# Last two of sixteen experts: rows of the sums fetched ahead, adds on VectorE, and the last expert in two groups of columns

## The chip, the cores and the metric

The kernel runs on one core of a Trainium2 chip. Time is device time in microseconds for one launch. TensorE (PE) does matrix products, VectorE (DVE) and ScalarE (ACT) work on elements, GpSimd (POOL) here mostly issues indirect DMAs, and SyncE (SP) issues loads. Each engine runs its instructions in the order in which the program lists them, and waits at one whose inputs aren't ready.

## The reference

One decoder layer on 2048 tokens of width 1024: a mixer (pooling and gated linear attention), then a mixture of 16 small experts. The change touches only the second half:

```python
def hier_moe(x, w_rg, b_rg, w_re, b_re, w_gate, w_up, w_down):
    ...   # each token: one group of 4 experts, two experts of that group, two weights
    for e in range(N_EXPERTS):
        h = jax.nn.silu(xt @ w_gate[e]) * (xt @ w_up[e])
        y = y + combine[:, e:e + 1] * (h @ w_down[e]).astype(f32)
    return y
# then, after h = h + hier_moe(rmsnorm(h)):
    return rmsnorm(h, final_norm_w)[:, N_META:]
```

Each expert has 256 hidden values. Both experts of a token are in the same group of four, so its row is complete after the later one of the two; then comes the final norm (a sum of squares over the row, a reciprocal root, a scaling) and the store.

## The kernel before, in words

Experts run one after the other, `e` from 0 to 15. Each takes up to 320 tokens (`CAP`), in three blocks of rows: `j` = 0 and 1 of 128 tokens, `j` = 2 of 64. As columns of the transposed tokens they stand in the order 2, 0, 1: columns 0 to 64, 64 to 192, 192 to 320 (`cols`). All values are split in a high and a low part, so that each product is three matmuls.

An expert has these steps. `gate_up`: for each half `f` of the hidden values, 8 blocks of 3 matmuls for the gate and 8 for the up matrix, 128 hidden values by 320 tokens each. The four sums go to PSUM banks: gate of `f` 0, up of `f` 0 and gate of `f` 1 to the tag `mm`, which has two banks taken in turn, up of `f` 1 to the tag `m2`, which has one. Then ScalarE does Silu into the one tile `h`, VectorE multiplies by the up sum, and `split_hidden` makes the high part (ScalarE) and the low part (VectorE) in `HB`. `down`: six units, one for each block `j` and half `a` of the 1024 outputs, each three matmuls of 512 columns for each `f` (two for `j` = 2 before the last expert, which packs its parts); first all units for `f` 0, then all for `f` 1. `evac` brings each unit into the row tile `xr`.

The running sums of the tokens lie in a DRAM array, `oe`. Before the change experts 0 to 14 do it thus: ScalarE copies the unit with the token's weight; an indirect DMA adds the rows of those tokens for which this expert is the first to `oe`; another adds the rows of `oe` to the tile, for those for which it is the second. `square` (ScalarE) sums the squares, `finish` takes the reciprocal root by a seed and three Newton steps on VectorE (`seed_rstd`, L51 to L67) and scales the row (L997), and `store` writes it to the output. Expert 15 is second for all its tokens: its three row tiles are fetched from `oe` while its gate products run (`between`, i = 1), and `evac` (L969) multiplies and adds on VectorE. Expert 14 is finished row block by row block (`finish_row`) from `between` of expert 15 (i = 4). For blocks 0 and 1 of expert 15, GpSimd multiplies by the final norm's weight (L1018) and ScalarE by the reciprocal root (L1023); block 2 goes through VectorE (L997).

There are six row tiles `xr` (`RB`), three for an expert, so that expert 15 takes those of expert 13 once these are stored. The order on each engine is made by a scheduler when the program is built, from dependences and priorities. The parts in `tc.high_priority()` are to be placed early; where they stand in the end only the list of the engine's instructions tells.

Of the kernel before, what the change touches and what calls it, by code (L numbers as in the profile page):

```python
# [7 lines left out]
F32 = mybir.dt.float32  # L8
F32R = mybir.dt.float32r
BF = mybir.dt.bfloat16  # L10
I32 = mybir.dt.int32
AF = mybir.ActivationFunctionType
# [57 lines left out]
def body(ctx, tc, I, O):  # L70
# [760 lines left out]
    with ExitStack() as c2:  # L831
# [54 lines left out]

        def gate_up(e, between):
            for f in range(2):
                ps = []
                for b in range(2):  # L890
                    p = bank(("mm", "m2")[f * b])
                    c = slice(b * 256 + f * 128, b * 256 + f * 128 + 128)
                    for k in range(KB):
                        if k % 4 == 0:
                            between(f * 4 + b * 2 + k // 4)
                        wh, wl = gate_slot(e, k)[0][:, c], gate_slot(e, k)[1][:, c]
                        xh, xl = XE[e % 2][k]
                        nc.tensor.matmul(p[:, :CAP], wh, xh, start=(k == 0), stop=False)  # L898
                        nc.tensor.matmul(p[:, :CAP], wh, xl, start=False, stop=False)  # L899
                        nc.tensor.matmul(p[:, :CAP], wl, xh, start=False, stop=(k == KB - 1))  # L900
                    ps.append(p)
                with tc.high_priority():
                    h = me.tile([128, CAP], F32, name="h")
                    nc.scalar.activation(h, ps[0][:, :CAP], AF.Silu)
                    V.tensor_tensor(h, ps[1][:, :CAP], h, op=OP.mult)
                    split_hidden(HB[:, f], h, 0, CAP)

# [34 lines left out]
        def down(e, js=(0, 1, 2)):  # L942
            le = e % 4
            if e < NE - 1 and e not in RT:
                RT[e] = [row_tile(True) for j in range(3)]
            tags = ("sp", "o", "ds", "tp", "zg", "m2") if e else ("mm", "mm", "ds", "m2", "ds", "m2")
            units = [(j, a, bank(tags[2 * j + a])) for j in js for a in range(2)]

# [15 lines left out]
            def evac(u):  # L964
                j, a, p = u
                n, c = rows[j], slice(a * 512, a * 512 + 512)
                x, w = RT[e][j][:n, c], col(e, j, 3, True)
                if e == NE - 1:
                    V.scalar_tensor_tensor(x, p[:n], w, x, op0=OP.mult, op1=OP.add)  # L969
                else:  # L970
                    nc.scalar.activation(x, p[:n], AF.Copy, scale=w)  # L971
                if j == 2 and e < NE - 1:
                    V.scalar_tensor_tensor(x, p[64:128], w, x, op0=OP.mult, op1=OP.add)
                x = RT[e][j]
                if a and le < 3:
                    add_oe(e, ind(oe, x[:n], col(e, j, 1), True, add=True), False)
                if a and le and e < NE - 1:
                    add_oe(e, ind(x[:n], oe, col(e, j, 2), False, add=True), True)
                if a and e == NE - 1:
                    finish_row(e, j)  # L980
# [32 lines left out]
        def finish_row(e, j):  # L1013
            n, x = rows[j], RT[e][j]
            square(e, j)
            if e == NE - 1 and j < 2:
                z = row_tile()
                nc.gpsimd.tensor_tensor(z[:n], x[:n], fw[:n], op=OP.mult)  # L1018
            ms = mk.tile([128, 1], F32, name="msl", bufs=3)
            V.scalar_tensor_tensor(ms[:n], SS[e % 2][:n, part[j]:part[j] + 1], SCALE / D, col(e, j, 4, True), op0=OP.mult, op1=OP.add)  # L1020
            r = seed_rstd(nc, mk, ms[:n], 1, n)
            if e == NE - 1 and j < 2:
                nc.scalar.activation(z[:n], z[:n], AF.Copy, scale=r)  # L1023
                store(e, j, z)
            else:
                scale_out(e, j, r)

# [24 lines left out]
        fw = mk.tile([128, D], F32, name="fw")  # L1052
        must_follow(nc.sync.dma_start(fw, I["fnw"].partition_broadcast(128)), first_rows)
        SS = [mk.tile([128, 3], F32, name=f"SS{i}") for i in range(2)]
        for i in range(2):
# [15 lines left out]
        for e in range(NE):  # L1071
            def between(i):
# [7 lines left out]
                else:  # L1080
                    for _ in range((e + 1 < NE) + (i < 4)):
                        gate = stream[done[0]][0] == "g"
                        for op in split_chunk():
                            if gate:
                                must_follow(op, hidden_done)
                        load_chunks(done[0] + WRB, mk)
                if e == NE - 1 and i == 1:
                    RT[e] = [row_tile(True) for j in range(3)]
                    for j, n in enumerate(rows):
                        add_oe(e, ind(RT[e][j][:n], oe, col(e, j, 0), False), True)  # L1090
                if i == 4 and e == NE - 1:
                    for j in range(3):
                        finish_row(e - 1, j)
            if e > 1:
# [147 lines left out]
```

## Time and profile before

| | us |
|---|---|
| median of 3 runs (1138.27 to 1140.39) | 1139.0 |
| the profiled execution | 1135.03 |
| its span, from the first to the last instruction | 1133.3 |
| TensorE busy, whole span | 1084.9 |
| VectorE busy, whole span | 790.1 |
| ScalarE busy, whole span | 583.3 |
| GpSimd busy, whole span | 290.8 |

The span is made of very different stages, so the busy times of the whole say little on its end. The profile's timeline gives each instruction's start, its duration, its line and tiles, and in brackets how long the engine stood idle ahead of it and what ended that. TensorE's matmuls overlap, so that the step from one start to the next is what one costs, not its duration. The granted clock of TensorE (PEclk) is 1.00 at 2.4 GHz and 0.50 at 1.2 GHz.

### The profile page before, as it was taken

To read this page: it belongs to the slowest core of one execution; us is meant where nothing else is said; L and a number is where in the kernel's file an instruction comes from. 1 tells how busy PE (TensorE), PEld (TensorE's weight loads), DVE (VectorE), ACT (ScalarE), POOL (GpSimd) and SP (SyncE) were. 2 spreads that over 40 slices of the span, in tenths; PEclk is the share of its full clock that TensorE was granted. 3 is DMA by queue.
4 is the path that set the end of the run, shared out by engine and by line. 5 is a ranking of instruction groups with operands and counts; after the bars stand their busy time and mean duration, and the time that the engine had idled before them with its cause. 6 is when DMAs were issued, how large, how long until landed. Compare 5 with 4: busy or idle time off the path is not lost. (4 is left out here: it accounts for less than half of the span.)

```text
span 1133.3 us, 19603 instructions
## 1 busy us (share of the span) xinstructions
PE 1084.9 (96%) x6748; PEld 974.0 (86%) x6748; DVE 790.1 (70%) x2706; ACT 583.3 (51%) x1286; POOL 290.8 (26%) x261
## 2 busy tenths in 40 slices
PE   6999999999999999999999997999999999999991
PEld 4888888888888889999999996679999889999980
DVE  6476666545554876777887887567886778688664
ACT  7545444344434733333333434477775777677541
POOL 2000000000000000111111126336645645564363
PEclk9999999999999999999999999999999999999996
DMA  7412323111211542343343535598999899799532
GB/s 267 172 66 75 117 89 102 48 56 62 69 66 57 177 158 99 127 150 141 112 150 103 178 134 175 166 307 209 245 270 258 215 275 288 181 254 275 155 72 75
DMA packets 75576, 175.41 MB, mean 155 GB/s; under 512 B 15283, under 2 KB 15716, under 8 KB 75472
## 3 DMA queue, kind: packets, MB, share of 16 engines
q1 hardware_dynamic: 48848, 105.73, 29.2%
q0 software_dynamic: 24032, 59.83, 20.1%
q10 hardware_dynamic: 2592, 8.55, 1.9%
q8 instruction: 55, 0.90, 0.3%
q14 instruction: 49, 0.40, 0.1%
HBM read 142.96 MB, written 52.76 MB: 173 GB/s over the span
## 5 line engine op out<-in xcount | busy, mean ns | idle before, releaser
L420 POOL DMA_DIRECT2D y_dram<-y x16 | 8.6, 540 | 392.7 <-DVE y L418 392.7
L849 POOL DMA_INDIRECT oe<-xr,tab x36 | 59.2, 1643 | 97.9 <-ACT xr L971 91.0
L300 PE MATMUL mm<-wb,XL 128*128 128x512 f32 (+1 forms) x240 | 83.6, 348 | 0.0
L301 PE MATMUL mm<-wb,XH 128*128 128x512 f32 (+1 forms) x240 | 83.1, 346 | 0.0
L299 PE MATMUL mm<-wb,XH 128*128 128x512 f32 (+1 forms) x240 | 82.3, 343 | 0.0
L653 POOL DMA_INDIRECT table<-rec,ix x32 | 33.5, 1045 | 179.6 <-DVE sv_all L669 142.8
L499 PE MATMUL mm<-XH,ws 128*128 128x256 f32 (+1 forms) x256 | 73.3, 287 | 0.1
L500 PE MATMUL mm<-XL,ws 128*128 128x256 f32 (+1 forms) x256 | 72.9, 285 | 0.0
L501 PE MATMUL mm<-XH,ws 128*128 128x256 f32 (+1 forms) x256 | 72.4, 283 | 0.0
L849 POOL DMA_INDIRECT xr<-oe,tab x36 | 57.6, 1599 | 22.9 <-ACT xr L971 12.8
L110 DVE TENSOR_TENSOR wb<-raw,wb 128x512 fp32r<-128x512 f32 x83 | 55.4, 686 | 9.4 <-ACT wb L109 8.5
L109 ACT ACTIVATE XH<-xt 128x1024 fp32r<-128x1024 f32 x32 | 33.9, 1058 | 49.4 <-PE mm L501 26.4
L109 ACT ACTIVATE wb<-raw 128x512 fp32r<-128x512 f32 x91 | 55.1, 624 | 4.4 <-DVE ix L636 1.8
L898 PE MATMUL mm<-xh,ws 128*128 128x320 f32 x168 | 53.4, 318 | 0.0
L900 PE MATMUL mm<-xh,ws 128*128 128x320 f32 x168 | 53.0, 316 | 0.0
L899 PE MATMUL mm<-xl,ws 128*128 128x320 f32 x168 | 52.6, 313 | 0.0
L991 ACT ACTIVATE sq<-xr 128x1024 bf16<-128x1024 f32 (+1 forms) x36 | 37.8, 1049 | 22.5 <-DMA xr<-oe,tab 8.1
L299 PE MATMUL mm<-ws,XH 128*128 128x512 f32 x112 | 47.4, 423 | 2.0 <-ACT XH L109 2.0
L299 PEld LDWEIGHTS mm<-wb,XH 128*128 128x128 f32 x240 | 45.3, 189 | 4.4
L301 PEld LDWEIGHTS mm<-wb,XH 128*128 128x128 f32 x240 | 45.2, 188 | 4.5
L300 PEld LDWEIGHTS mm<-wb,XL 128*128 128x128 f32 x240 | 45.2, 189 | 4.3
L499 PEld LDWEIGHTS mm<-XH,ws 128*128 128x128 f32 x256 | 47.9, 188 | 0.9 <-ACT XH L109 0.6
(615 smaller groups left out, 3946.6 us busy)
## 6 DMA issues: line engine op xcount, KB each, us to landing
raw<-in_wgu_e_dram SPq DMA_DIRECT2D x86, 256.0 KB
xt<-in_xT_dram SPq DMA_DIRECT2D x32, 512.0 KB
xn<-in_xn_dram SPq DMA_DIRECT2D x32, 512.0 KB
raw<-in_wd_e_dram SPq DMA_DIRECT2D x48, 256.0 KB
wr<-in_wgu_e_dram SPq DMA_DIRECT2D x42, 256.0 KB
hn_dram<-xn ACTq DMA_DIRECT2D x16, 512.0 KB
oe<-xn POOLq DMA_DIRECT2D x16, 512.0 KB
raw<-in_wrest_dram SPq DMA_DIRECT2D x16, 256.0 KB
```

Source lines behind the costliest of these rows:

```text
L109: return (nc.scalar.activation(hi, src, AF.Copy), (eng or V).tensor_tensor(lo, src, hi.bitcast(F32), op=OP.subtract))
L110: (eng or V).tensor_tensor(lo, src, hi.bitcast(F32), op=OP.subtract))
L299: nc.tensor.matmul(q, xh[:, k, :], wh[:, c0:c1_], start=(k == 0), stop=False)
L300: nc.tensor.matmul(q, xl[:, k, :], wh[:, c0:c1_], start=False, stop=False)
L301: nc.tensor.matmul(q, xh[:, k, :], wl[:, c0:c1_], start=False, stop=(k == KB - 1))
L499: nc.tensor.matmul(ps[:, b], WS[k][0][:, c], XH[:, k, o:], start=(k == 0), stop=False)
L500: nc.tensor.matmul(ps[:, b], WS[k][0][:, c], XL[:, k, o:], start=False, stop=False)
L501: nc.tensor.matmul(ps[:, b], WS[k][1][:, c], XH[:, k, o:], start=False, stop=(k == KB - 1))
L849: return nc.gpsimd.indirect_dma_start(out=out_, out_offset=off if scatter else None, in_=in_, in_offset=None if scatter else off, bounds_c ...
L898: nc.tensor.matmul(p[:, :CAP], wh, xh, start=(k == 0), stop=False)
L899: nc.tensor.matmul(p[:, :CAP], wh, xl, start=False, stop=False)
L900: nc.tensor.matmul(p[:, :CAP], wl, xh, start=False, stop=(k == KB - 1))
```

## The change

Experts 14 and 15 (`ahead`) now both fetch their rows of `oe` into the row tiles ahead of their `down`, and `evac` multiplies and adds on VectorE (L971 of the changed kernel). Expert 14 then writes the rows for which it is the first to `oe` as they are, without adding, and no longer reads `oe` back. The squares of both are taken by half rows in `evac` (L984), into `SL`. `finish_row` adds the halves and scales on VectorE for all blocks; the multiplication on GpSimd is gone. Expert 15 goes through `gate_up` by columns: first 0 to 192 (blocks 2 and 0) for both `f`, then 192 to 320 (block 1) for `f` 0, then `down` of blocks 0 and 2, then columns 192 to 320 for `f` 1, and `down` of block 1.

```diff
-        def gate_up(e, between):
-            for f in range(2):
+        def gate_up(e, between, fs=(0, 1), c0=0, c1_=CAP):
+            for f in fs:
...
-                        xh, xl = XE[e % 2][k]
-                        nc.tensor.matmul(p[:, :CAP], wh, xh, start=(k == 0), stop=False)
+                        xh, xl = (x[:, c0:c1_] for x in XE[e % 2][k])
+                        nc.tensor.matmul(p[:, c0:c1_], wh, xh, start=(k == 0), stop=False)
...
                 with tc.high_priority():
                     h = me.tile([128, CAP], F32, name="h")
-                    nc.scalar.activation(h, ps[0][:, :CAP], AF.Silu)
-                    V.tensor_tensor(h, ps[1][:, :CAP], h, op=OP.mult)
-                    split_hidden(HB[:, f], h, 0, CAP)
+                    nc.scalar.activation(h[:, c0:c1_], ps[0][:, c0:c1_], AF.Silu)
+                    V.tensor_tensor(h[:, c0:c1_], ps[1][:, c0:c1_], h[:, c0:c1_], op=OP.mult)
+                    split_hidden(HB[:, f], h, c0, c1_)
...
             tags = ("sp", "o", "ds", "tp", "zg", "m2") if e else ("mm", "mm", "ds", "m2", "ds", "m2")
+            tags = ("sp", "o", "ds", "sp", "zg", "tp") if e == NE - 1 else tags
+            ahead = e >= NE - 2
...
-                if e == NE - 1:
+                if ahead:
                     V.scalar_tensor_tensor(x, p[:n], w, x, op0=OP.mult, op1=OP.add)
                 else:
                     nc.scalar.activation(x, p[:n], AF.Copy, scale=w)
...
                 if a and le < 3:
-                    add_oe(e, ind(oe, x[:n], col(e, j, 1), True, add=True), False)
-                if a and le and e < NE - 1:
+                    add_oe(e, ind(oe, x[:n], col(e, j, 1), True, add=not ahead), False)
+                if a and le and not ahead:
                     add_oe(e, ind(x[:n], oe, col(e, j, 2), False, add=True), True)
+                if ahead:
+                    h = slice(a * 512, a * 512 + 512)
+                    sq = mk.tile([128, D], BF, name="sq")
+                    nc.scalar.activation(sq[:n, h], RT[e][j][:n, h], AF.Square, accum_out=SL[e % 2][:n, j, a:a + 1])
...
         def finish_row(e, j):
-            n, x = rows[j], RT[e][j]
-            square(e, j)
-            if e == NE - 1 and j < 2:
-                z = row_tile()
-                nc.gpsimd.tensor_tensor(z[:n], x[:n], fw[:n], op=OP.mult)
-            ms = mk.tile([128, 1], F32, name="msl", bufs=3)
-            V.scalar_tensor_tensor(ms[:n], SS[e % 2][:n, part[j]:part[j] + 1], SCALE / D, col(e, j, 4, True), op0=OP.mult, op1=OP.add)
-            r = seed_rstd(nc, mk, ms[:n], 1, n)
-            if e == NE - 1 and j < 2:
-                nc.scalar.activation(z[:n], z[:n], AF.Copy, scale=r)
-                store(e, j, z)
-            else:
-                scale_out(e, j, r)
+            n, q = rows[j], SL[e % 2][:rows[j], j]
+            ms = mk.tile([128, 1], F32, name="msl", bufs=3)[:n]
+            V.tensor_scalar(ms, q[:, 0:1], q[:, 1:2], SCALE / D, op0=OP.add, op1=OP.mult)
+            V.tensor_tensor(ms, ms, col(e, j, 4, True), op=OP.add)
+            scale_out(e, j, seed_rstd(nc, mk, ms, 1, n))
...
-                if e == NE - 1 and i == 1:
+                if e >= NE - 2 and i == 1 and e not in RT:
                     RT[e] = [row_tile(True) for j in range(3)]
                     for j, n in enumerate(rows):
                         add_oe(e, ind(RT[e][j][:n], oe, col(e, j, 0), False), True)
-                if i == 4 and e == NE - 1:
-                    for j in range(3):
-                        finish_row(e - 1, j)
+                if i == 4 and e == NE - 1 and e - 1 not in OUT:
+                    OUT[e - 1] = [finish_row(e - 1, j) for j in range(3)]
+            if e == NE - 1:
+                gate_up(e, between, (0, 1), 0, 192)
+                gate_up(e, between, (0,), 192, CAP)
+                down(e, (0, 2))
+                gate_up(e, between, (1,), 192, CAP)
+                down(e, (1,))
+                break
```

How the built order moves is seen in the lists of instructions. In them `h` is the tile of hidden values, `HB` its split, `msl` and `sr_y` belong to the reciprocal roots, `mm` and `m_...` are the banks of gate and up, `sp`, `o`, `ds` are banks of `down`; the numbers behind a name tell buffers apart.

VectorE, the first hidden values of expert 15, before: they stand behind the conversion of the last down weights and the first step of one reciprocal root.

```order
L110 TENSOR_TENSOR wb_105<-wr,wb_104 128x512
L1020 SCALAR_TENSOR_TENSOR msl<-SS_8915,tab 128x1
L905 TENSOR_TENSOR h<-mm,h 128x320
L58 TENSOR_SCALAR sr_y<-msl 128x1
L59 TENSOR_SCALAR sr_y<-sr_y 128x1
```

The same place after the change:

```order
L66 SCALAR_TENSOR_TENSOR sr_y<-sr_t,sr_y 64x1
L1003 SCALAR_TENSOR_TENSOR xr<-xr,sr_y,fw 64x1024
L905 TENSOR_TENSOR h<-mm,h 128x192
L883 TENSOR_TENSOR HB<-h,HB 128x128
L885 TENSOR_TENSOR HB<-h,HB 128x64
L905 TENSOR_TENSOR h<-m_13546,h 128x192
```

The first multiplication now stands behind the whole end of expert 14: the row that scales its last block (64x1024) is the one ahead of it. Between the last split of expert 14's hidden values and this multiplication stand 60 instructions: 8 adds, 4 conversions, 6 scalings and 42 small ones.

TensorE, the end of expert 15's gate and up products, before: `down` follows at once.

```order
L898 MATMUL m_13535<-xh_8712,wb_100 128x320
L899 MATMUL m_13535<-xl_8713,wb_100 128x320
L900 MATMUL m_13535<-xh_8712,wb_101 128x320
L957 MATMUL sp<-wb_102,HB 128x512
L958 MATMUL sp<-wb_102,HB 128x512
```

After, at the end of the first group of columns:

```order
L898 MATMUL m_13546<-xh_8712,wb_100 128x192
L899 MATMUL m_13546<-xl_8713,wb_100 128x192
L900 MATMUL m_13546<-xh_8712,wb_101 128x192
L898 MATMUL mm<-wb_106,wb_94 128x128
L899 MATMUL mm<-wb_107,wb_94 128x128
```

Two sums of 128 columns, 48 matmuls, now stand between the first group's hidden values and `down`, and the first of them takes the `mm` bank that the first up sum of the group was in.

VectorE near the end, before: the six units of `down` come one after the other, with the roots among them.

```order
L969 SCALAR_TENSOR_TENSOR xr<-ds,tab,xr 128x512
L969 SCALAR_TENSOR_TENSOR xr<-tp,tab,xr 128x512
L1020 SCALAR_TENSOR_TENSOR msl<-SS_8916,tab 128x1
L969 SCALAR_TENSOR_TENSOR xr<-zg,tab,xr 64x512
L58 TENSOR_SCALAR sr_y<-msl 128x1
```

After, the last hidden values and the last two units:

```order
L1003 SCALAR_TENSOR_TENSOR xr<-xr,sr_y,fw 64x1024
L905 TENSOR_TENSOR h<-m_13731,h 128x128
L883 TENSOR_TENSOR HB<-h,HB 128x128
L971 SCALAR_TENSOR_TENSOR xr<-ds,tab,xr 128x512
L971 SCALAR_TENSOR_TENSOR xr<-sp,tab,xr 128x512
L1022 TENSOR_SCALAR msl<-SL_8916 128x1
```

The last hidden multiplication stands behind the scaling of blocks 0 and 2, and only block 1 is left behind it.

## Rows read from the trace of the kernel before

**Rows 1.** Windows, whole core: from:to, length; busy us (count) by engine; clock, DMA
```profile
1082.43:1096.70 14.27, 14.21 (x97) 13.94 (x95) 9.34 (x21) 5.77 (x11) 12.13 (x8) 1.00 0.48 65
1096.70:1108.90 12.20, 10.44 (x36) 7.16 (x36) 10.95 (x32) 3.76 (x10) 10.06 (x9) 0.86 0.60 177
1099.70:1102.90 3.20, 3.20 (x9) 2.51 (x9) 2.92 (x11) 0.92 (x2) 2.69 (x2) 0.51 0.51 140
1108.90:1120.45 11.55, 0.00 (x0) 0.00 (x0) 9.26 (x30) 4.44 (x6) 6.60 (x5) 0.69 0.18 66
```
**Rows 2.** Timeline of TensorE, experts 14 and 15: start, duration, instruction [idle before]
```profile
1079.19 0.40 PE L959 MATMUL sp<-wb,HB 128*128 128x512 f32 x1
...
1082.43 0.31 PE L898 MATMUL mm<-wb,wb 128*128 128x320 f32 x1
...
1096.33 0.31 PE L900 MATMUL m<-xh,wb 128*128 128x320 f32 x1
...
1098.96 0.50 PE L958 MATMUL sp<-wb,HB 128*128 128x512 f32 x1 [1.08 <-DVE HB L883]
...
1104.56 0.39 PE L957 MATMUL sp<-wb,HB 128*128 128x512 f32 x1
...
1108.49 0.40 PE L959 MATMUL m<-wb,HB 128*64 128x512 f32 x1
```
**Rows 3.** Timeline of ScalarE: squares of expert 14 and expert 15
```profile
1090.76 1.06 ACT L991 ACTIVATE sq<-xr 128x1024 bf16<-128x1024 f32 x1 [4.18 <-DMA xr<-oe,tab]
...
1106.98 1.06 ACT L991 ACTIVATE sq<-xr 128x1024 bf16<-128x1024 f32 x1 [3.41 <-DVE xr L969]
```
**Rows 4.** Timeline of VectorE from 1080 us on
```profile
1080.76 0.17 DVE L1008 SCALAR_TENSOR_TENSOR ms<-SS,tab 128x3 f32<-128x3 f32 x1 [0.35 <-ACT sq L991]
...
1083.16 1.29 DVE L997 SCALAR_TENSOR_TENSOR xr<-xr,sr_y,fw 128x1024 f32<-128x1024 f32 x1
...
1085.82 2.47 DVE L997 SCALAR_TENSOR_TENSOR xr<-xr,sr_y,fw 128x1024 f32<-128x1024 f32 x2
1088.20 1.29 DVE L110 TENSOR_TENSOR wb<-raw,wb 128x512 fp32r<-128x512 f32 x2
...
1092.13 0.49 DVE L905 TENSOR_TENSOR h<-mm,h 128x320 f32<-128x320 f32 x1
...
1105.47 0.73 DVE L969 SCALAR_TENSOR_TENSOR xr<-sp,tab,xr 128x512 f32<-128x512 f32 x1
1106.14 0.75 DVE L969 SCALAR_TENSOR_TENSOR xr<-o,tab,xr 128x512 f32<-128x512 f32 x1
...
1108.69 3.81 DVE L1020 SCALAR_TENSOR_TENSOR msl<-SS,tab 128x1 f32<-128x1 f32 x1
...
1113.81 0.13 DVE L59 TENSOR_SCALAR sr_y<-sr_y 128x1 int32<-128x1 int32 x1
...
1117.09 1.28 DVE L997 SCALAR_TENSOR_TENSOR xr<-xr,sr_y,fw 64x1024 f32<-64x1024 f32 x1
```
**Rows 5.** Timeline of GpSimd: a gather with addition, the multiplications, the last store
```profile
1084.03 1.85 POOL L849 DMA_INDIRECT xr<-oe,tab  x1 [0.30 <-issue]
...
1107.78 4.70 POOL L1018 TENSOR_TENSOR xg<-xr,fw 128x1024 f32<-128x1024 f32 x2
...
1119.53 0.92 POOL L849 DMA_INDIRECT out_dram<-xr,tab  x1 [0.30 <-issue]
```
**Rows 6.** DMA, 1055 to 1080 us: busy tenths in 40 slices of 0.625 us
```profile
DMA  7998668996799897559775410000000000000000
```
**Rows 7.** Timeline of TensorE earlier: 128 columns at full clock, 256 at half
```profile
199.73 0.39 PE L389 MATMUL o<-v,sc 128*128 128x128 f32 x2
...
200.18 0.39 PE L389 MATMUL o<-v,sc 128*128 128x128 f32 x2
...
8.63 0.41 PE L294 MATMUL tp<-ws,XM 128*16 128x256 f32 x1
8.85 0.63 PE L301 MATMUL zg<-ws,XH 128*128 128x512 f32 x1
```

More of the change, by code (lines that the diff above doesn't have):

```diff
@@ L896, in gate_up @@
                         wh, wl = gate_slot(e, k)[0][:, c], gate_slot(e, k)[1][:, c]
-                        xh, xl = XE[e % 2][k]
-                        nc.tensor.matmul(p[:, :CAP], wh, xh, start=(k == 0), stop=False)
-                        nc.tensor.matmul(p[:, :CAP], wh, xl, start=False, stop=False)
-                        nc.tensor.matmul(p[:, :CAP], wl, xh, start=False, stop=(k == KB - 1))
+                        xh, xl = (x[:, c0:c1_] for x in XE[e % 2][k])
+                        nc.tensor.matmul(p[:, c0:c1_], wh, xh, start=(k == 0), stop=False)
+                        nc.tensor.matmul(p[:, c0:c1_], wh, xl, start=False, stop=False)
+                        nc.tensor.matmul(p[:, c0:c1_], wl, xh, start=False, stop=(k == KB - 1))
                     ps.append(p)
@@ L943, in down @@
             le = e % 4
-            if e < NE - 1 and e not in RT:
+            if e not in RT:
                 RT[e] = [row_tile(True) for j in range(3)]
             tags = ("sp", "o", "ds", "tp", "zg", "m2") if e else ("mm", "mm", "ds", "m2", "ds", "m2")
+            tags = ("sp", "o", "ds", "sp", "zg", "tp") if e == NE - 1 else tags
+            ahead = e >= NE - 2
             units = [(j, a, bank(tags[2 * j + a])) for j in js for a in range(2)]
@@ L1053, in body @@
         must_follow(nc.sync.dma_start(fw, I["fnw"].partition_broadcast(128)), first_rows)
+        SL = [mk.tile([128, 3, 2], F32, name=f"SL{i}") for i in range(2)]
         SS = [mk.tile([128, 3], F32, name=f"SS{i}") for i in range(2)]
@@ L1080, in between @@
                 else:
-                    for _ in range((e + 1 < NE) + (i < 4)):
+                    for _ in range(min((e + 1 < NE) + (i < 4), len(stream) - done[0])):
                         gate = stream[done[0]][0] == "g"
```

## Prediction

> **What bounds the kernel now.** I read the windows first, cut at the places where TensorE changes its work, then TensorE's timeline to find its gaps, then the chain of waits and the timelines of VectorE, GpSimd and ScalarE from 1075 us on. The change touches nothing that any engine does before the second half of expert 14, so only this end counts. In the windows the reader is to see three different stretches, and a piece of the second by itself [rows 1]. From 1082.43 to 1096.70 TensorE is full (14.21 of 14.27 us): the 96 gate and up products of expert 15. From 1096.70 to 1108.90 it does 36 products of the down matrix in 12.20 us, at a mean clock of 0.86. From 1108.90 to 1120.45 TensorE does nothing, and VectorE, ScalarE and GpSimd finish three row blocks. Behind that lie the landing of the last rows and the program's exit, which the change leaves alone.
>
> TensorE's timeline says why the second stretch is long [rows 2]: the first down products wait for the hidden values (1.08 us at the second), and then the clock is at 0.51 for 3.2 us, half of the 2.4 GHz, in which it does 9 products [rows 1]; at the 0.231 us of the later ones it would be 14. The hidden values are late since ScalarE and VectorE first work on the end of expert 14: ScalarE's square waits 4.18 us for rows that a DMA adds up [rows 3], and the copy of the hidden values stands behind it. In the third stretch the reader is to see a VectorE instruction of one element per partition that takes 3.81 us [rows 4]: it lies beside GpSimd's two multiplications of 4.70 us together [rows 5], and everything behind it on VectorE is held.
>
> The last GpSimd instruction ends at 1119.53 + 0.92 = 1120.45 [rows 5]. I work out when it ends in the changed kernel; what lies behind it is taken as the same. The profiled execution took 1135.03 us, the median of the runs shown is 1139.0; I add the difference to the median.
>
> **Expert 14: adds on VectorE.** Gone are the six copies with a factor on ScalarE, three accumulating gathers on GpSimd's queue and the wait for them. New are three gathers ahead and six (with the second halves of block 2, eight) adds of 0.67 us on VectorE (1105.47 to 1106.14) [rows 4]. The gathers must follow expert 13's additions. All transfers of that time are over at 1069.4 (23 of 40 slices of 0.625 us from 1055 on), and the DMA engines are idle from there to 1080 [rows 6]. An accumulating gather landed 6.7 us after its issue began (1084.03 to 1090.76) [rows 3, 5]. So the first is there at about 1076.1, the third, two issues of 1.85 us later, at about 1079.8; they are needed from 1079.6 and 1082.3 on. I cost this at nothing; the idle DMA stretch is its cover. If it fell short, each microsecond late would move everything below by one.
>
> TensorE hands over the first finished sum at 1079.19 + 0.40 = 1079.6 [rows 2]. In the changed order VectorE now has, between that add and the first hidden value of expert 15, 60 instructions without a wait of their own that is late: 8 adds at 0.67 = 5.4; 4 conversions of the last down weights at 0.65 (1.29 for two) = 2.6; 6 scalings of whole rows (experts 13 and 14) at 1.19 (1085.82 to 1088.20 for two) = 7.1; and 42 small instructions of four reciprocal roots (12 for expert 13's three blocks together, 10 for each block of 14). A small one costs 0.20 us where each needs the one before (12 from 1080.76 to 1083.16) and 0.13 where two chains are mixed (25 from 1113.81 to 1117.09) [rows 4]. The list has both kinds; I take 0.16, so 6.7 (5.5 to 8.4). Sum 21.8 us: the first hidden multiplication of expert 15 starts at 1101.4 (1100.2 to 1103.1). In the kernel before it stood in front of nearly all this and started at 1092.13 [rows 4]. Here a stall goes, the wait for the gathered sums, and what comes late in its place is the hidden values: VectorE has no idle time left to give, yet the order puts them last.
>
> **Expert 15: two groups of columns.** Before, 96 products 320 wide, every 0.1463 us (1082.43 to 1096.33, 95 steps) [rows 2]. Now 96 are 192 wide and 96 are 128 wide. Products of 128 with a new weight block each follow one another every 0.1125 us (four from 199.73 to 200.18) [rows 7]; 192 isn't shown. From below, the line through 320 and 512 (0.231: 17 steps from 1104.56 to 1108.49 [rows 2]) gives 0.089 at 192 and 0.060 at 128. I take 0.1125 for both, the row of the same width: each product has its weight load of 128 columns, however few tokens it takes.
>
> The Trainium skill, "TensorE: Matmul & The Clock Gate", section "Back-to-back issue gap", states a sustained 81 ns for N=128 with a weight load each. This trace has 112.5, so the rule is too quick here; by it the 48 products below would take 3.9 us and the forecast would be 1.5 us lower.
>
> So the first group (96 products) ends at 1082.4 + 10.8 = 1093.2. The next 48 (first hidden half, last 128 columns) need a PSUM bank. The tag mm has two banks; first-half gate and up took both, second-half gate takes the first again after ScalarE's Silu, and the next user of the other one must wait until VectorE has multiplied out of it. That is the instruction of 1101.4, and with an estimated 0.35 us (0.49 for 320 columns [rows 4]) the bank is free at 1101.8. TensorE, in order, stands still for 8.6 us; behind the waiting product are queued all down products. The 48 then take 5.4 us (2.9 to 5.4). After the pause of 1.08 us the clock was at half for 3.2 us [rows 1, 2]; a pause of 8.6 us will not do less. At half clock a product of 256 columns took 0.22 us (8.63 to 8.85) [rows 7]; one of 128 lies between 0.1125 and that, which costs 0 to 1.55 us in such a stretch. I take 1.5, since that row is the only one at half clock. The down products of blocks 0 and 2 start at T = 1101.8 + 5.4 + 1.5 = 1108.7.
>
> **From T to the end.** 24 products at 0.231: 5.55; last add to 6.4 (0.73 and a hop); two mixed roots, 16 small at 0.16: 9.0; scaling 1.19: 10.2; 4 small at 0.20: 11.0; scaling: 12.2. Only here does the order put the second hidden half of block 1. Its products (48 at 0.1125, T + 5.6 to T + 11.0) are long done, and so is half of block 1's down work. Multiplication, copy and subtraction of 128 columns, an estimated 0.3 each (0.49 and less for 320): 13.1. Five products and the drain: 14.45. Add: 15.2. The square is now of 512, an estimated 0.7 with its read (1.06 for 1024 [rows 3]): 15.9. Ten small at 0.20: 17.9. Scaling 1.28: 19.2. Store, 0.3 and 0.92 as the last one before: T + 20.4.
>
> From the last product to the last store that is some 6 us where it was 11.6, so the end itself gains over 5 us: no GpSimd multiplication, no held VectorE, one block in place of three. It is not enough. 1108.7 + 20.4 = 1129.1 against 1120.45 is +8.7 us: 1143.7 for the profiled execution, 1147.7 by the median. With all bounds low (1100.2; 2.9; no half clock; 0.13 for the mixed ones of the 30 small instructions) the end is 1123.1, +2.6, 1141.6; with all high (1103.1; 5.4; 1.55; 0.20) 1131.5, +11, 1150.
>
> **Rivals.** *The hidden values aren't held.* If VectorE were through by about 1091, TensorE would run on: T = 1082.4 + 144 x 0.1125 = 1098.6, the end 1119.0, -1.4 us: 1137.6, no change. For it: the finishing of 14 begins some 4 us earlier than before. Against it: even at the lowest prices the list is 20.6 us long, and it would have to be 11.
>
> *The same, with cheap narrow products: faster.* Place: the bank mm ahead of the 48 products. With 0.089 and 0.060 the 144 take 11.4 us, T = 1093.8, the end 1114.2, -6.2 us: 1132.8. It decides from the point where the bank is free before 1094.6 (1120.45 - 20.4 - 5.4), 7.2 us sooner than I expect. Against it the row of 0.1125 too.
>
> *More than one stall.* The half clock lasts through all 48 products (0.22 each, 3.7 us more than in the sum), or the gathers for 14 land late (VectorE's list starts later by as much), or both: 1151.4 to 1155. For it: no pause in these rows is as long as 8.6 us, and the gathers have only 2.5 to 3.5 us to spare. Against it: the idle DMA engines, and the 3.2 us of the stretch shown.
>
> *The stall is there, but small:* prices near the low ends, 1141.3 to 1143.
>
> **How the numbers follow.** The forecast, 1143 to 1151, has 0.75; more than one stall 0.10; small stall 0.06; not held 0.06; cheap and not held 0.03. A difference under 0.2% (2.3 us) can't be told from no change in this kernel. So slower 0.91 (the first three), same 0.06, faster 0.03. The range 1142.5 to 1152 leaves out the two last cases and parts of the two before them.
>
> **What would show it.** In the profile after: (1) VectorE busy without a gap from 1079.6 to about 1101, the first 192-wide multiplication at its end; (2) TensorE idle from about 1093 to 1102 in front of the first 128-wide product, released by VectorE; (3) 0.11 us between narrow products, and half clock behind the gap; (4) no wait for gathers at 1079.6; (5) the second hidden half of block 1 behind two row scalings; (6) about 6 us from last product to last store. I would be wrong if the multiplication starts before 1095 or if TensorE doesn't wait for it; if only (3) is off, the sign stays.

## The result and the profile after

The changed kernel took 1149.7 us (median of 4 runs, 1148.52 to 1152.34) against 1138.63 us for the kernel before beside it (1134.44 to 1140.39): ratio 1.0104, 95% interval 1.0078 to 1.0129. It is about 11 us slower. The forecast was 1147.7 us, in a range of 1142.5 to 1152.0. Later, beside the experiments below, the same kernel gave 1145.09 against 1132.21 us, ratio 1.0117 (1.0094 to 1.0140).

The profiled execution took 1148.52 us (span 1146.8; before 1135.03 and 1133.3). The gate products of expert 15 start at 1083.41 us, 0.98 us later than before [rows 2], and the last store ends at 1133.02 + 0.97 = 1133.99 us against 1120.45 [rows 5]. So this last stage, from the first gate product of expert 15 to the end of the last store, takes 50.58 us where it took 38.02. These 12.56 us and the later start make up the 13.5 us between the two profiled executions; by the medians the loss is 11.1 us. I call the stage the end stage below and compare the experiments by it too, since the start of expert 15 moves by some microseconds from run to run.

The windows of the changed kernel, cut where TensorE changes its work; columns as in [rows 1], whose rows they answer to:

```profile
1083.41:1094.20 10.79, 10.79 (x97) 10.69 (x95) 10.75 (x37) 4.27 (x13) 6.04 (x4) 1.00 0.10 34
1094.20:1100.88 6.68, 0.07 (x2) 0.00 (x1) 6.35 (x22) 0.02 (x1) 5.46 (x5) 0.82 0.34 100
1100.88:1111.18 10.30, 10.30 (x49) 10.30 (x49) 1.21 (x5) 1.31 (x4) 3.30 (x4) 0.50 0.48 148
1111.18:1115.53 4.35, 4.35 (x12) 2.87 (x12) 0.58 (x2) 0.31 (x1) 0.00 (x0) 0.51 0.00 0
1115.53:1134.00 18.47, 11.92 (x75) 9.60 (x73) 13.09 (x41) 4.92 (x14) 2.86 (x3) 0.96 0.14 44
```

The busy columns are TensorE's products, its weight loads, VectorE, ScalarE and GpSimd. Read the first two of them and the clock. The 96 products of 192 columns fill 10.79 us. Then TensorE does almost nothing for 6.68 us. Then 48 products of 128 columns take 10.30 us at a clock of 0.50, the lower of its two levels (1.2 GHz), and the half clock goes on for ten products of the down matrix (4.35 us). VectorE, the third busy column, is full in the first two windows and nearly idle in the next two: it held TensorE up, and afterwards waits for it.

TensorE's timeline has the wait and what ends it, and the return of the clock:

```profile
1093.99 0.27 PE L900 MATMUL m<-xh,wb 128*128 128x192 f32 x1
1100.88 0.47 PE L898 MATMUL mm<-wb,wb 128*128 128x128 f32 x1 [6.61 <-DVE h L905]
1101.15 0.41 PE L899 MATMUL mm<-wb,wb 128*128 128x128 f32 x1
...
1111.18 0.73 PE L959 MATMUL sp<-wb,HB 128*128 128x512 f32 x1
1111.71 0.63 PE L960 MATMUL sp<-wb,HB 128*128 128x512 f32 x1
...
1115.53 0.39 PE L960 MATMUL tp<-wb,HB 128*64 128x512 f32 x1
...
1127.22 0.39 PE L961 MATMUL sp<-wb,HB 128*128 128x512 f32 x1
```

On VectorE the instruction that frees the bank (line 905, the first hidden multiplication of expert 15) stands behind the whole end of expert 14, without a gap from 1080.59 on. Before, it started at 1092.13 [rows 4]: expert 13's root and scalings, two additions and the conversions stood ahead of it there too, but of expert 14's three roots and scalings only one small instruction. Measured from the first gate product, it starts 17.06 us in, where it was 9.70:

```profile
1080.59 0.75 DVE L971 SCALAR_TENSOR_TENSOR xr<-sp,tab,xr 128x512 f32<-128x512 f32 x1 [2.80 <-PE sp L961]
...
1090.50 3.67 DVE L1003 SCALAR_TENSOR_TENSOR xr<-xr,sr_y,fw 128x1024 f32<-128x1024 f32 x3
...
1099.16 1.28 DVE L1003 SCALAR_TENSOR_TENSOR xr<-xr,sr_y,fw 64x1024 f32<-64x1024 f32 x1
1100.47 0.36 DVE L905 TENSOR_TENSOR h<-mm,h 128x192 f32<-128x192 f32 x1
...
1123.97 1.28 DVE L1003 SCALAR_TENSOR_TENSOR xr<-xr,sr_y,fw 64x1024 f32<-64x1024 f32 x1
1125.18 0.28 DVE L905 TENSOR_TENSOR h<-m,h 128x128 f32<-128x128 f32 x1
```

The last store on GpSimd, which answers to the end of [rows 5]; it ends 6.38 us behind the last product, where before it was 11.56:

```profile
1133.02 0.97 POOL L849 DMA_INDIRECT out_dram<-xr,tab  x1 [6.58 <-DVEq L1119]
```

### The profile page after: what moved, and what is told of

Its sections match the earlier page's. It is cut to its first block, busy times and chain, and to the rows that moved or that the text cites. A ratio compares the mean times of both kernels' runs of the same rounds, so it can differ in the third digit from the quotient of the medians.

```text
span 1146.8 us, 19830 instructions
## 1 busy us (share of the span) xinstructions
PE 1099.2 (96%) x6844; PEld 988.7 (86%) x6844; DVE 790.4 (69%) x2724; ACT 580.5 (51%) x1294; POOL 283.1 (25%) x259
## 5 line engine op out<-in xcount | busy, mean ns | idle before, releaser
L849 POOL DMA_INDIRECT xr<-oe,tab x36 | 54.6, 1516 | 25.3 <-ACT xr L973 12.8
L849 POOL DMA_INDIRECT out_dram<-xr,tab x36 | 44.8, 1245 | 38.2 <-DVE sr_t L62 18.4
L898 PE MATMUL mm<-wb,wb 128*128 128x320 f32 (+2 forms) x144 | 45.7, 317 | 6.6 <-DVE h L905 6.6
```

Source lines behind the costliest of these rows:

```text
L849: return nc.gpsimd.indirect_dma_start(out=out_, out_offset=off if scatter else None, in_=in_, in_offset=None if scatter else off, bounds_c ...
L898: nc.tensor.matmul(p[:, c0:c1_], wh, xh, start=(k == 0), stop=False)
```

## The experiments

Theory: VectorE's list holds the bank mm, TensorE waits, and the half clock behind the wait costs as much again; the other parts of the change gain. The main rivals are that the column groups, or the rows ahead, cost by themselves. Each kernel was timed beside runs of the kernel before on the same chip; "against before" is the difference of those medians. On the chips of the experiments the kernel before took 1131.7 to 1132.8 us, so the whole times in the expectations, which start from 1138.6, are to be read as differences from it. The end stage is read from one profiled execution of each kernel. The two of the changed kernel differ by 0.8 us, so I build nothing on a difference of that size.

Result of each kernel:

| kernel | us against before | ratio (95%) | end stage, us |
|---|---|---|---|
| before | 0 | 1 | 38.02 |
| changed | +11.1 and +12.9 | 1.0104, 1.0117 | 50.58, 49.78 |
| no column groups | -6.4 | 0.9937 (0.9919 to 0.9955) | 32.56 |
| other banks | +1.9 | 1.0016 (0.9999 to 1.0034) | 40.39 |
| list behind | -1.7 | 0.9978 (0.9966 to 0.9989) | 38.11 |
| busy gap | +4.4 | 1.0034 (1.0017 to 1.0050) | 43.68 |
| groups alone | +11.1 | 1.0109 (1.0082 to 1.0136) | 49.11 |
| VectorE end alone | -2.6 | 0.9976 (0.9963 to 0.9988) | 35.51 |
| blocks in two turns | -4.8 | 0.9959 (0.9941 to 0.9978) | 31.76 |
| wide products behind | +8.8 | 1.0091 (1.0061 to 1.0121) | 45.71 |
| block 0 on GpSimd | -2.5 | 0.9978 (0.9959 to 0.9997) | 33.75 |

**Other banks.** The edit gives the 48 products banks that VectorE emptied long before:

```
-                    p = bank(("mm", "m2")[f * b])
+                    p = bank(("ds", "tp")[b] if c0 and f == 0 else ("mm", "m2")[f * b])
```

> The changed kernel with one edit: the 48 products of 128 columns that follow the 192-column group write the banks ds and tp, which VectorE emptied long before, and not mm. VectorE's list and its order stay. Theory: no product waits for the hidden multiplication any more, the 48 run at full clock at 0.112 us each between 1094 and 1099.6 us of the span, the down products start behind the hidden values at about 1101.5 instead of 1111.2: 9 to 10 us faster than the changed kernel, 1140 us (1137 to 1143), about the kernel before. Rival, the columns in two groups cost by themselves (more and narrower products, more small instructions on ScalarE and VectorE): within 3 us of the changed kernel, 1147 to 1150 us.

The end stage fell by 10.2 us against the changed kernel (50.58 to 40.39; by 9.4 from its second profile), and the ratio went from 1.0104 to 1.0016: 1.9 us over the kernel before, where +1.4 (-1.6 to +4.4) was expected. The windows show the 48 products at full clock right behind the first group, then the down products:

```profile
1078.88:1089.56 10.68, 10.68 (x97) 10.68 (x96) 10.63 (x36) 4.27 (x13) 6.00 (x3) 1.00 0.10 34
1089.56:1094.95 5.39, 5.39 (x50) 5.37 (x49) 5.14 (x22) 0.00 (x0) 4.41 (x4) 1.00 0.22 60
1096.75:1101.29 4.54, 4.54 (x12) 2.84 (x13) 1.78 (x7) 1.28 (x4) 2.92 (x3) 0.62 0.84 266
```

The timelines of VectorE and TensorE show the hidden multiplication and the wait:

```profile
1095.94 0.36 DVE L905 TENSOR_TENSOR h<-mm,h 128x192 f32<-128x192 f32 x1
...
1096.75 0.50 PE L959 MATMUL sp<-wb,HB 128*128 128x512 f32 x1 [1.68 <-ACT HB L881]
```

VectorE's list did not change, and the hidden values came as late as in the changed kernel (17.06 us behind the first gate product in both). Yet TensorE used the time for the 48 products and waited only 1.68 us, for ScalarE's copy of the hidden values. Behind that short wait the clock fell too: it is 0.62 over the first 12 down products. The bank, not the list as such, was the cost. The rival that stays within 3 us of the changed kernel falls.

**List behind.** The first instruction of each block's finishing (expert 14) is queued behind the first group's hidden values, and the finishing is written there:

```
...
+            if behind[0]:
+                queued_after(s_, behind[0])
...
-                if i == 4 and e == NE - 1 and e - 1 not in OUT:
-                    OUT[e - 1] = [finish_row(e - 1, j) for j in range(3)]
...
                 gate_up(e, between, (0, 1), 0, 192)
+                behind[0] = hidden_done[0]
+                for j in range(3):
+                    finish_row(e - 1, j)
+                behind[0] = None
```

> The changed kernel with VectorE's list for expert 14 (means of squares, roots, three scalings) put behind the hidden values of the 192-column group of expert 15, written and queued; banks as in the changed kernel. Theory: the bank mm comes free at about 1090 us of the span as soon as ScalarE and VectorE are there, TensorE waits for nothing, the half clock does not appear, the down products start at about 1100; the list then stands ahead of the additions of expert 15 and ends at about 1108 us: 1139 us (1136 to 1143). Rival, the list costs wherever it stands, since VectorE is the bound there: 1145 us or more. Rival, the narrow products cost by themselves: 1147 us or more.

The wait for the bank shrank to 0.21 us, and no half clock followed. The end stage is 12.5 us shorter than in the changed kernel (11.7 by its second profile), and the time is 1.7 us under that of the kernel before where +0.4 was expected (-2.6 to +4.4). TensorE at the end of the first group and of the 48 products:

```profile
1090.34 0.33 PE L898 MATMUL mm<-wb,wb 128*128 128x128 f32 x1 [0.21 <-DVE h L905]
...
1095.75 0.45 PE L959 MATMUL sp<-wb,HB 128*128 128x512 f32 x1
1096.04 0.40 PE L960 MATMUL sp<-wb,HB 128*128 128x512 f32 x1
```

The same work in another order on one engine is worth 12.5 us here. Compare the end stages, though: 38.11 us is what the kernel before has. Freed of the stall, the whole change gains next to nothing.

**Busy gap.** 28 useless products of 512 columns fill the wait; the bank and VectorE's list stay as they are:

```
+                p = bank("o")
+                for i in range(N_IDLE):
+                    nc.tensor.matmul(p, XE[e % 2][0][0][:, 0:128], gate_slot(e, 0)[0], start=True, stop=True)
```

> The changed kernel with 28 useless products of 512 columns between the two groups (6.5 us at full clock, in the gap in which TensorE waits for the bank). The wait for the bank stays. Theory: the gap is what takes the clock down; with TensorE busy in it the 48 products of 128 columns run at 0.112 us instead of 0.213 (4.9 us less) and the first down products at 0.23 instead of 0.43 (2 us less): 1143 us (1141 to 1145). Rival, the granted clock falls for another reason (narrow products, the load of the other engines): 1148 to 1151 us, and the 48 still at 0.213 us.

The end stage fell by 6.9 us (6.1 from the second profile), as worked out (4.9 + 2.0), and the time is 4.4 us over that of the kernel before, as expected (1143 from 1138.6). The windows are the 28 products, the 48 products and the first 24 down products, all at a clock of 1.00:

```profile
1088.02:1094.79 6.77, 6.70 (x31) 5.12 (x29) 6.43 (x23) 0.02 (x1) 5.50 (x5) 1.00 0.34 96
1094.79:1100.15 5.36, 5.36 (x48) 5.36 (x49) 1.22 (x5) 1.31 (x4) 3.30 (x4) 1.00 0.86 276
1100.15:1105.70 5.55, 5.55 (x26) 3.92 (x26) 2.36 (x5) 1.27 (x4) 0.00 (x0) 1.00 0.04 10
```

So the half clock came with TensorE's pause: once the pause is filled, nothing else in this stage brings it. With the bank held as long as in the changed kernel, 6.9 of the 12.6 us are the clock alone. The other 5.7 us (43.68 against 38.02) are the pause and what the groups cost, less what the rest of the change gains.

**No column groups.** The changed kernel with expert 15 in 320 columns as before:

```
-            tags = ("sp", "o", "ds", "sp", "zg", "tp") if e == NE - 1 else tags
...
-            if e == NE - 1:
-                gate_up(e, between, (0, 1), 0, 192)
-                gate_up(e, between, (0,), 192, CAP)
-                down(e, (0, 2))
-                gate_up(e, between, (1,), 192, CAP)
-                down(e, (1,))
-                break
```

> The changed kernel without the two groups of columns: expert 15 is multiplied in 320 columns as before; the rows fetched ahead, the additions on VectorE and the end without GpSimd's multiplication stay. Theory (the loss is the mm bank held by the group of 192 columns till VectorE's list for expert 14 is through, and the half clock behind it; the other two parts gain): the first hidden multiplication of 320 columns stands early in VectorE's list, TensorE does not wait for it, and the end on VectorE alone gains some 5 us: 1133 us (1130 to 1137). Rival, the rows ahead and the longer VectorE list cost by themselves: 1143 us or more.

Expected was 5.6 us less than the kernel before (1133 from 1138.6), measured 6.4. The windows are the gate and up products, the down products and the end:

```profile
1077.99:1092.03 14.04, 14.04 (x97) 14.04 (x96) 13.97 (x52) 5.29 (x15) 7.95 (x6) 1.00 0.15 47
1092.03:1100.55 8.52, 8.52 (x38) 5.93 (x36) 7.16 (x16) 2.36 (x6) 6.53 (x6) 1.00 0.65 205
1100.55:1110.55 10.00, 0.00 (x0) 0.00 (x0) 8.54 (x36) 2.45 (x8) 2.85 (x3) 0.72 0.26 93
```

TensorE is full for 22.56 us without a wait. The 96 products of 320 columns take 14.04 us. In groups the 192 products take 10.79 + 5.36 + 5.31 = 21.46 us at full clock (5.36 in the kernel with the busy gap, 5.31 for the last 48 in the changed kernel), 7.4 us more for the same result. The shorter end behind the last product (6.4 in place of 10.0 us) gives back 3.6. The groups lose even where nothing waits; the kernel with the list behind, which has them, stands 5.6 us of end stage behind this one. By its median this is also the fastest version measured, faster than both kernels; blocks in two turns (below) can't be told from it.

**Groups alone, and the VectorE end alone.** The first is the kernel before plus the groups; the second is the kernel before with one edit:

```
-            if e == NE - 1 and j < 2:
-                z = row_tile()
-                nc.gpsimd.tensor_tensor(z[:n], x[:n], fw[:n], op=OP.mult)
...
-            if e == NE - 1 and j < 2:
-                nc.scalar.activation(z[:n], z[:n], AF.Copy, scale=r)
-                store(e, j, z)
-            else:
-                scale_out(e, j, r)
+            scale_out(e, j, r)
```

> The kernel before with the two groups of columns alone: the rows of the sums still added by DMA, the end still with GpSimd's multiplication. Theory: VectorE's list for expert 14 stands before the first hidden multiplication here too, and now it waits for the added rows as in the kernel before, so the bank mm is held till about 1103 us (worked out from the kernel before: squares of its third block at 1098, root 1.6 us, scaling 1.3 us, one more pair for the second block), the half clock takes 5 us in the 48 products and 2 us behind them, and the end after the last product is the long one of 11.6 us: 17 to 22 us slower than the kernel before. Rival, the loss in the change comes from the rows ahead or the longer VectorE end: at most 8 us slower.

> The kernel before with one edit: the last expert's blocks are scaled on VectorE, and GpSimd multiplies nothing. Theory: GpSimd's 4.7 us and ScalarE's scaling behind it go from the end, VectorE's root and scaling of 64 rows become the last: 4 us faster than the kernel before (2 to 5), and the rest of what the changed kernel without column groups gained (6 to 7 us) belongs to the rows fetched ahead. Rival, the whole gain of that kernel is the VectorE end: 6 to 7 us faster here as well. Rival, the rows ahead are what gained: no change here.

The end on VectorE alone gives 2.6 us (end stage 2.51), where 4 (2 to 5) was expected: both rivals of the second expectation fall. If the parts add up, 3 to 4 us of the kernel without groups (6.4 less 2.6, or 5.46 less 2.51 by the end stage) belong to the rest of the change: rows ahead, additions on VectorE, squares by half rows. The groups alone lost 11.1 us: less than the 17 to 22 worked out, more than the 8 that the rival allows. The sign was right and the place was wrong, and the end behind the last product took 7.48 us, not 11.6. There the wait of TensorE lies in the middle of the first group, on ScalarE's Silu, which stands behind a square that waits 4.28 us for added rows. ScalarE's timeline:

```profile
1092.27 1.06 ACT L992 ACTIVATE sq<-xr 128x1024 bf16<-128x1024 f32 x1 [4.28 <-DMA xr<-oe,tab]
1093.23 0.19 ACT L992 ACTIVATION_READ_ACCUMULATOR sq<-xr 128x1 f32 x1
1093.32 0.31 ACT L904 ACTIVATE h<-mm 128x192 f32<-128x192 f32 x1
```

and TensorE's in the same kernel, with the half clock gone at 1097.4:

```profile
1093.69 0.53 PE L898 MATMUL mm<-wb,wb 128*128 128x192 f32 x1 [9.12 <-ACT h L904]
...
1097.21 0.41 PE L899 MATMUL mm<-wb,wb 128*128 128x192 f32 x1
1097.43 0.32 PE L900 MATMUL mm<-wb,wb 128*128 128x192 f32 x1
1097.59 0.27 PE L898 MATMUL mm<-xh,wb 128*128 128x192 f32 x1
```

The theory has no place for what follows. A longer pause (9.1 us) was followed by only 3.7 us at half clock, with products of 192 columns; in the changed kernel 6.6 us of pause were followed by 14.65 us, with products of 128.

**Wide products behind the wait.** The products of the second group take 192 columns, 64 of them for nothing: the 48 behind the wait, and the 48 of the other hidden half later, which run at full clock:

```
+            m0 = c0 - 64 if c0 else 0
...
-                        xh, xl = (x[:, c0:c1_] for x in XE[e % 2][k])
-                        nc.tensor.matmul(p[:, c0:c1_], wh, xh, start=(k == 0), stop=False)
...
+                        xh, xl = (x[:, m0:c1_] for x in XE[e % 2][k])
+                        nc.tensor.matmul(p[:, m0:c1_], wh, xh, start=(k == 0), stop=False)
...
```

> The changed kernel, but the products of the second column group (128 columns) take 192 columns: 64 columns of the first group are multiplied once more into a bank area that nobody reads. Count of products, bank, wait and VectorE's list stay; each product only has more to do. Theory (the width of the products behind the wait decides how long the half clock stays: in the kernel with groups alone, products of 192 columns follow a longer wait and the clock was back after some 3 us, in the changed kernel products of 128 columns follow and it stayed down for 14 us): a few products at 0.213 us, then 0.112 us each, the down products all at 0.23 us; 5 to 6 us faster than the changed kernel, 5 to 8 us slower than the kernel before. Rival, the half clock lasts for a time set by the wait or by what the other engines do: all 48 at 0.213 us as in the changed kernel, 10 to 13 us slower than before.

The wait is the same to the last digit (6.61 us), and each product takes the same 0.213 us at half clock; but the clock is back after some 20 of them, and the 24 down products behind them all run at full clock:

```profile
1097.06 0.53 PE L899 MATMUL mm<-wb,wb 128*128 128x192 f32 x1 [6.61 <-DVE h L906]
...
1101.22 0.33 PE L900 MATMUL mm<-xl,wb 128*128 128x192 f32 x1
...
1102.29 0.28 PE L900 MATMUL mm<-wb,wb 128*128 128x192 f32 x1
...
1104.52 0.42 PE L960 MATMUL sp<-wb,HB 128*128 128x512 f32 x1
1104.78 0.40 PE L961 MATMUL sp<-wb,HB 128*128 128x512 f32 x1
```

The end stage is 4.9 us shorter than in the changed kernel's first profile, 4.1 than in its second: a kernel that computes more is done sooner. The times point the same way (1.0091 against 1.0117), but their intervals overlap, and 8.8 us over the kernel before lies between the 5 to 8 expected and the 10 to 13 of the rival. So the profile carries this, one execution of it. With the pause and VectorE's list unchanged, the half clock was shorter where wider products followed, and groups alone (3.7 us, 192 columns) agrees. The rival, a length set by the pause or by the other engines, falls.

**Blocks in two turns, and block 0 on GpSimd.** Both start from the kernel without groups; the first multiplies blocks 0 and 2 by the down matrix before block 1 and fetches the rows into free buffers, the second adds one multiplication on GpSimd, with the scaling behind it on ScalarE:

```
...
+            if e == NE - 1:
+                down(e, (0, 2))
-            down(e, (0, 1, 2) if e else (1,))
+            down(e, (0, 1, 2) if 0 < e < NE - 1 else (1,))
```

```
+            if e == NE - 1 and j == 0:
+                z = row_tile()
+                nc.gpsimd.tensor_tensor(z[:n], RT[e][j][:n], fw[:n], op=OP.mult)
...
```

> The changed kernel without column groups (320 columns in every gate product), with the down products of expert 15 in two turns, blocks 0 and 2 first and block 1 last, and its rows of the sums fetched in the order 0, 2, 1 into buffers that stand free instead of those that the stores of expert 13 release. Theory: the narrow products are what the groups cost on TensorE (about 8 us more than 320 columns) and only the end with one block left is worth having, which needs no narrow products: the last product stands as in the kernel without groups, and the end behind it is 6.4 us instead of 9.6: 3 us faster than that kernel (1.5 to 3.5), 9 to 10 us faster than the kernel before. Rival, the end is set by VectorE's additions and roots and not by the last product: no gain over the kernel without groups, 6 to 7 us faster than before.

> The kernel with rows ahead, no column groups and the down products in two turns, with one edit: the first of the last expert's blocks is multiplied by the norm's weights on GpSimd and scaled on ScalarE, the other two on VectorE. Theory: the end of that kernel is VectorE's list (six additions, three roots, three scalings), no longer a transfer or the last product; taking one scaling of 1.28 us off it ends the kernel 1 to 1.5 us earlier, 6 to 8 us faster than the kernel before. Rival, GpSimd's multiplication slows VectorE beside it and takes the gain back: 4 to 5 us faster than before, as without it.

The first missed: 4.8 us faster than before, not to be told from the 6.4 without it, and the end behind the last product is still 9.21 us, not 6.4. Its rival has the mechanism, if not its 6 to 7 us: VectorE's list of additions, roots and scalings is what ends there. VectorE is at it almost without a gap from the end of expert 14 to the last scaling, which its timeline shows:

```profile
1095.13 1.28 DVE L1002 SCALAR_TENSOR_TENSOR xr<-xr,sr_y,fw 64x1024 f32<-64x1024 f32 x1
1096.33 0.73 DVE L970 SCALAR_TENSOR_TENSOR xg<-sp,tab,xg 128x512 f32<-128x512 f32 x1
...
1106.95 1.28 DVE L1002 SCALAR_TENSOR_TENSOR xg<-xg,sr_y,fw 128x1024 f32<-128x1024 f32 x1
```

The second missed too: 2.5 us faster than before, less even than the 4 to 5 of its rival, and its end stage is 2.0 us longer than without GpSimd (33.75 against 31.76). The rival's mechanism is there. VectorE's timeline of that kernel, and GpSimd's:

```profile
1100.90 0.20 DVE L1024 TENSOR_SCALAR msl<-SL 128x1 f32<-128x1 f32 x1
1101.13 3.00 DVE L1025 TENSOR_TENSOR msl<-msl,tab 128x1 f32<-128x1 f32 x1
1104.06 0.74 DVE L970 SCALAR_TENSOR_TENSOR xg<-ds,tab,xg 128x512 f32<-128x512 f32 x1
```

```profile
1101.73 2.38 POOL L1022 TENSOR_TENSOR xg<-xg,fw 128x1024 f32<-128x1024 f32 x1
```

The addition of one element per partition takes 3.00 us, against 0.14 for the same line elsewhere, and ends with GpSimd's multiplication (1104.13 and 1104.11). To save 1.28 us, VectorE was held for 2.9. The 3.81 us of [rows 4] beside the 4.70 us of [rows 5] look the same, and end together too (1112.50 and 1112.48). The Trainium skill, "SBUF — State Buffer", section "SBUF: two separate sides", says that the two engines share a pair of ports, and that a VectorE instruction with two inputs in SBUF and a GpSimd instruction that reads SBUF block each other: the one that starts first keeps the pair for its whole length. This trace agrees with the blocking (3.00 against 0.14 us). It does not bear out the order: by the profile, whose times on GpSimd are rough, VectorE's instruction starts 0.60 us ahead of the multiplication and is held all the same.

**The changed kernel once more.**

> The changed kernel once more, beside the others on the same chip: 10 to 13 us slower than the kernel before, the 48 products at 0.213 us each behind a wait of 6 to 7 us. Nothing is told apart by it; it gives the size of the change on this chip.

A wait of 6.61 us again, the 48 products in 10.30 us at 0.50, then six down products at half clock, and 12.9 us lost:

```profile
1096.45:1106.75 10.30, 10.30 (x48) 10.30 (x49) 1.21 (x5) 1.31 (x4) 3.30 (x4) 0.50 0.45 146
1106.75:1109.40 2.65, 2.65 (x7) 1.98 (x8) 0.58 (x2) 0.31 (x1) 0.00 (x0) 0.50 0.00 0
```

## Why the prediction was right, and which term was not

- *Rows ahead cost nothing*: right. VectorE's first addition of expert 14 waits for TensorE (2.80 us, on the product), not for a gather. The gathers began later than worked out (1071.81 against 1069.4; [rows 6] has 24 slices with transfers, not 23), but were on time. That they and the additions gain 3 to 4 us where nothing else is in the way was not seen; it follows from two kernels (no column groups, VectorE end alone), not from one edit.
- *VectorE's list of 21.8 us*: right in its order, 1.9 us too long. It took 19.9 us (1080.59 to 1100.47) without a gap. In the mixed chains a small instruction starts 0.07 to 0.13 us behind the one before it, where 0.16 was taken. One reading was wrong: the multiplication did not stand in front of nearly all of this list before. Of the 60 instructions 22 stood ahead of it there, and the other additions were ScalarE's copies. Against the first gate product it moved by 7.4 us, where the sum has 9.3 (1092.13 to 1101.4).
- *Products of 192 and 128 columns at 0.1125 us*: right. 10.79 us for 96, and 5.36 for 48 at full clock in the kernel with the busy gap. The width makes no difference at this clock; 192 columns had not been shown before.
- *The wait for the bank, released by the hidden multiplication*: right. 6.6 us against 8.6, since the list was shorter; the later start moved both ends of the wait alike. Other banks and the list behind take it away, and nearly all the loss with it.
- *The half clock, 1.5 us*: this term was mis-sized. It was taken to last the 3.2 us of [rows 1], and only the rival "more than one stall" let it last through the 48 products. It lasted 14.65 us: 10.30 instead of 6.9 us for the 48 products (+3.4 against the sum), and 4.35 instead of 2.31 us for the next ten (+2.0). The 3.2 us came from a place where products of 512 columns followed; here products of 128 did, and the kernel with the wide products shows that their width matters (4.2 us with 192 columns). Products of 512 behind so long a pause were not tried. So one half of that rival came true, which I had given 0.10; the gathers, its other half, were on time. Its times, 1151.4 to 1155, were not reached, since the list was shorter.
- *T to the end, 20.4 us*: 22.8, the 2.0 us of clock in it. The hidden values of block 1 stand behind two scalings (1125.18) as forecast, and 6.38 us from the last product to the last store answer to "some 6".

Against the sum of 1129.1 the last store ended at 1133.99: +1.0 for the later start, -1.9 for the list, +5.4 for the clock, +0.4 in the end. Two errors of opposite sign partly met, so the time forecast is better than its terms. Luck helped once more: the profiled execution missed its forecast (1143.7) by 4.8 us, the median missed 1147.7 by only 2.0, since the profiled pair differs by 13.5 us and the medians by 11.1. The low end of the prediction's sum is also 0.3 us too low: its terms give 1123.4, not 1123.1.

Of the rivals, "not held" needed the list to be shorter by some 10 us, and "cheap and not held" by 7.2; it was shorter by 1.9. The kernel with the list behind is nearest to "not held" made true: its time was -1.7 us against the kernel before, where -1.4 was worked out. With other banks the bank is free but the hidden values stay late, and it was +1.9. "Small stall" fell with the 10.30 us.

The kernel with groups alone and the changed kernel lose nearly the same (11.1 us against 11.1 and 12.9), with their waits at different places. By their rows they meet by chance: the first has 2.5 us more of pause (9.12 against 6.61), 1.1 us more behind the last product (7.48 against 6.38), and some 5 us less of half clock. This adds up to the 1.5 us by which its end stage is shorter, but no edit separated these terms, so that stays open.

## What to carry to other kernels

When instructions move to an engine, look at what stood in front of the list and now stands behind it: a single small instruction that frees a PSUM bank can hold TensorE for the length of the whole list, and another bank or another order takes that away. Price a pause of TensorE twice, once for the wait and once for the half clock behind it, and read the second from a place where products of the same width follow: here 48 products of 128 columns stayed at half clock to the last, and some 20 of 192 did. Before splitting columns, multiply the count of products by the time of one at the new width: here 192 narrow ones cost 7.4 us more than 96 wide ones and shortened the end by 3.6.

## What the runs showed of the hardware that was not expected

- Products of 128 columns and of 192 follow each other every 0.111 us at full clock, and every 0.213 us at half clock, both with a weight block of 128 columns each.
- Behind a pause of 6.61 us the clock stayed at half for 14.65 us (13 us in the second profile) where 48 products of 128 columns followed, and for 4.2 us where 48 of 192 columns followed.
- A VectorE instruction on 128x1 took 3.00 us beside a GpSimd multiplication of 128x1024 (2.38 us), and 0.14 us without it.
